# One-bank attention steps held back and issued ahead of a three-bank step, in a two-layer hybrid encoder kernel on one core

## The chip, the core and the metric

The kernel runs on one core of a Trainium2 chip. The metric is device time in microseconds (us) of one execution, and the time of a kernel is the median of several. Five engines work side by side and each takes its own instructions in program order: PE (matrix products and transposes), DVE (vector work), ACT (scalar functions and copies), POOL and SP (which starts most transfers). Results of PE land in PSUM, which has eight banks.

## What is computed

Two layers run over 320 tokens: 256 of a prompt and the next 64 of a stream with a cache. Each layer has one combined projection, two kinds of attention of eight heads each, an output projection and a feed-forward block:

```
h   = x @ w_in                      # q, k, v of A and of B, and an indexer's q, k, w
A   = softmax(q k' / 8 + bias) v    # band of 64-frame chunks, learned relative bias
B   = the same over the 64 (prompt) or 80 (sample) keys that the indexer picks:
      score[t,s] = sum_h w[t,h] * relu(q_idx[t,h] . k_idx[s]),  top k of the admissible keys
x   = LayerNorm(alpha * x + concat(A, B) @ w_out)
x   = LayerNorm(alpha * x + relu(x @ w_up)^2 @ w_down)
```

All is float32. The outputs are the 320 rows of x and the new keys, values and indexer keys of both layers.

## The kernel before, in words

**Weight products.** Every weight arrives as units of 1024 x 128 numbers (`raw`, loaded by SP). ACT rounds a unit to a high part (`wh`, L184) and DVE subtracts it to get the low part (`wl`, L190). Tokens are split in the same way, and for each unit and each of eight slices of 128 inputs PE issues three products (L202, L203, L204: high x high, high x low, low x high) over all 320 tokens into a bank of a pool `mm`. There are 4776 of them. "Product 480" below means the point in PE's order after 480 of these, counted from the start of the program.

**Attention steps.** Each layer has eight pairs of heads, four of A (the code calls them with `flip`, or b0 to b3 in the output's order) and four of B. When the projections of a pair are there, its steps follow one another:

- value: three transposes (L333) into one bank, two copies by ACT (L334, L335).
- scores: six products (L399, L401) into three banks; DVE adds the bias and takes maxima (L419, L422); ACT takes exponentials (L427, "exps"); DVE and ACT divide by the sums (L432, L435, L437).
- turn: nine transposes (L451) into three banks, copied out by ACT (L455, L457, L458) or DVE (L453).
- output: twelve small products (L470, L473) into one bank, which the step finish empties: ACT rounds (L479), DVE subtracts (L480).
- dots and weigh (L541, L543, L518, L520) score keys for the indexer; DVE picks the best (L583, L585). Keys and queries of B are rotated by DVE first (L302 to L305).

These steps share a pool `at` of four banks, taken in turn, so that a step's bank is free once the reader of the bank's last user is done.

**What sets the order.** The program is written by a planner in Python, before anything runs. It has a clock that goes forward by 0.408 us after each three products. `later(dt, fn)` puts a step on an agenda at clock + dt with dt from a table WAIT (for layer 0, output 2.0, finish 4.0, value 5.2; for layer 1, 3.8, 3.2 and 9.2), and `advance` issues what is due, oldest first. A step that finds too few banks by the planner's count (`held`) is put off to the next slot. Issuing a step appends its instructions to the order of each engine that it uses: so the place of L479 in ACT's order and of L480 in DVE's follows from when the planner issues finish, and finish is due a fixed time after its output.

```
        later(WAIT[l]["finish"], self.finish, p)
...
        nc.scalar.activation(self.o[0], pv, AF.Copy)
        nc.vector.tensor_tensor(self.o[1], pv, self.o[0].bitcast(F32), op=ALU.subtract)
        release(1)
```

Of the kernel before, what the change touches and what calls it, by code (L numbers as in the profile page):

```python
# [44 lines left out]
N_WARM = 6  # L45
N_TAIL = 4
STORE = 10.0
TOKENS = slice(0, P), slice(P, 2 * P), slice(T - P, T)
WAIT = [{"lo": 3.4, "rope": 4.6, "scores": 3.4, "peaks": 0.0, "exps": 1.0, "normalise": 5.6, "turn": 3.0,
         "output": 2.0, "finish": 4.0, "value": 5.2, "keys": 6.0, "dots": 10.8, "clip": 0.0, "weigh": 0.2,  # L50
# [25 lines left out]
def encoder_step(ctx: ExitStack, tc: tile.TileContext, a: dict):  # L76
# [24 lines left out]
    held = [0]  # L101

    def side_banks(n, fn, *args):

        if held[0] + n > N_SIDE:
            later(NEXT, fn, *args)
            return None
        held[0] += n
        return [acc("at", N_SIDE) for _ in range(n)]

    def release(n):
        held[0] -= n

    def unit(dt=F32, w=T):
        return st([P, 3 * P], "u", N_UNIT, dt)[:, :w]
# [5 lines left out]
    clock = [0.0]  # L121
    agenda = []

    def later(dt, fn, *args):
        agenda.append((clock[0] + dt, len(agenda), fn, args))

    def advance(dt):
        clock[0] += dt
        while agenda:
            i = min(range(len(agenda)), key=lambda i: agenda[i][0])  # L130
            if agenda[i][0] > clock[0]:
                break
            _, _, fn, args = agenda.pop(i)
            fn(*args)

    def put(out, t):

        later(STORE, nc.sync.dma_start, out, t)

    def flush():  # L140
        while agenda:
            advance(NEXT)


# [29 lines left out]
    def prefetch(upto):  # L174

        while at["split"] <= min(upto, len(units) - 1):
            i = at["split"]
            while i not in raw:
                advance(NEXT)
            w = raw.pop(i)  # L180
            n = w.shape[2]
            hi = st([P, KD, P], "wh", 5, F32R)[:, :, :n]
            lo = st([P, KD, P], "wl", 5, F32R)[:, :, :n]
            nc.scalar.activation(hi, w, AF.Copy)  # L184
            split[i] = (hi, lo)
            at["split"] += 1
            later(WAIT[l]["lo"], split_rest, i, hi, lo, w)
# [7 lines left out]
    def until(ready):  # L195
        while not ready():
            advance(NEXT)
# [93 lines left out]
    def evacuate(dst, src, scale=1.0):  # L291
        s, b = src
        if b is None:
            nc.scalar.activation(dst, s, AF.Copy, scale=scale)  # L294
        elif scale != 1.0:
            nc.vector.tensor_scalar(dst, s, b, scale, op0=ALU.add, op1=ALU.mult)
        else:
            nc.scalar.activation(dst, s, AF.Identity, bias=b, scale=scale)
# [21 lines left out]
    def value(v, src, out, then):  # L320

        f = unit()
        evacuate(f, src)
        put(out, f)

        def turn():
            got = side_banks(1, turn)
            if not got:
                return
            pt = got[0]  # L330
            release(1)
            for c, n in ((0, P), (1, P), (2, TS)):
                nc.tensor.transpose(pt[:n, c * P:(c + 1) * P], f[:, c * P:c * P + n], ident)  # L333
            nc.scalar.activation(v[:, 0:2], pt[:, 0:2 * P].rearrange("p (c d) -> p c d", c=2), AF.Copy)  # L334
            nc.scalar.activation(v[:TS, 2], pt[:TS, 2 * P:3 * P], AF.Copy)  # L335
            then()

        later(WAIT[l]["value"], turn)

    def bias_tiles(l, j):  # L340

# [9 lines left out]
    def sample_blocks(f, at, keep):  # L351

        other = f[:, (at + 64 if keep == 0 else at - 64):][:, :64]
        here = f[:, at:at + 64]
        mine, rest = HALVES[keep][1], HALVES[1 - keep][1]
        nc.gpsimd.tensor_copy(other[rest], here[rest])
        nc.gpsimd.memset(here[rest], 0.0)
        nc.gpsimd.memset(other[mine], 0.0)

    class Pair:  # L360
# [18 lines left out]
        def got(self, what):  # L379
            self.have.add(what)  # L380
            if what == "q":
                sample_blocks(self.qf, 64 if self.flip else 2 * P, 1 if self.flip else 0)
            if what in "qk" and {"q", "k"} <= self.have:
                later(WAIT[l]["scores"], self.scores)
            if {"v", "p"} <= self.have:
                later(WAIT[l]["output"], self.output)

        def scores(self):
            if not self.add:
# [41 lines left out]
        def normalise(self):  # L431
            nc.vector.reciprocal(self.sums, self.sums)  # L432
            for i, (p, _, _) in enumerate(self.parts):
                if i < WAIT[l]["na" if self.flip else "nb"]:
                    nc.scalar.activation(p, p, AF.Copy, scale=self.sums[:, i:i + 1])  # L435
                else:
                    nc.vector.tensor_scalar(p, p, self.sums[:, i:i + 1], None, op0=ALU.mult)  # L437
            later(WAIT[l]["turn_a" if self.flip else "turn"], self.turn)

        def turn(self):  # L440
            banks = side_banks(3, self.turn)
# [42 lines left out]
    class Index:  # L484
# [40 lines left out]

        def got(self, j):
            sample_blocks(self.qf[j], 2 * P, 0)
            later(WAIT[l]["dots"], self.dots, j)

        def dots(self, j):  # L530

# [139 lines left out]
    class LastNorm(Norm):  # L671
# [20 lines left out]
        def finish(self, psum):  # L692
# [13 lines left out]
            def gather(c0, part, first=False, last=False):  # L706

                for i, t in enumerate(TOKENS):
                    nc.tensor.matmul(pc[:, c0 + i:c0 + i + 1], part[:, t], mean_w[:, 0:1], start=first and i == 0,
# [47 lines left out]
    for l in range(DEPTH):  # L757
# [4 lines left out]
        def take(name, j, src):  # L762
            if name == "ki":
                index.keys(src)
            elif name == "qi":
                roped(index.q[j], src, 0, None, lambda: index.got(j))
            else:
                p, kind, br = pairs[name[1], j], name[0], name[1]
                if kind == "v":
                    value(p.v, src, a["o_" + name][l, j], lambda: p.got("v"))  # L770
                elif br == "b":
                    roped(getattr(p, kind), src, 2 if kind == "q" else 0, a["o_kb"][l, j] if kind == "k" else None,
                          lambda: p.got(kind))
                elif kind == "q":
                    evacuate(p.q, (src[0][:, T - 1::-1], src[1]), scale=HD ** -0.5)
                    later(WAIT[l]["a"] - WAIT[l]["scores"] if kind == "k" else 0, p.got, kind)
                else:
                    evacuate(p.k, src)
                    put(a["o_ka"][l, j], p.k)
                    later(WAIT[l]["a"] - WAIT[l]["scores"] if kind == "k" else 0, p.got, kind)  # L780
# [68 lines left out]
        if not final:  # L849
# [9 lines left out]
            for k in range(0, KD, 2):  # L859
                later(WAIT[l]["renew"] + WAIT[l]["renew2"] * k, renew, k)  # L860
    flush()


# [88 lines left out]
```

## Time and profile before

| | before |
|---|---|
| median of 3 executions | 825.57 us (825.29 to 828.98) |
| the profiled execution | 827.0 us, span 824.2 us |
| PE busy | 815.2 us, 99% of the span |
| DVE busy | 604.5 us, 73% |
| ACT busy | 446.3 us, 54% |
| granted PE clock | full (1.00) in every stretch listed below |

The profile is of one execution; its span runs from the first to the last instruction, and the time lies 2.8 us above it. Busy shares are means over stages that differ much: DVE stands near 100% in some stretches of the attention and near 40% in the feed-forward blocks. The chain that ended last lies 93% on PE.

### The profile page before, as it was taken

Reading aid. Unit: us, or ns where it says so; the run is one execution under the profiler, and the core shown is the slowest. Engines: PE = TensorE matmul, PEld = TensorE weight load, DVE = VectorE, ACT = ScalarE, POOL = GpSimd, SP = SyncE. Lnnn points to the kernel's source line nnn. Section 1 sums busy time; section 2 is a strip of 40 time slices with the busy share of each in tenths; the row PEclk is TensorE's granted clock in tenths of the full one; section 3 lists DMA queues with packets and bytes.
Section 4 is the critical chain, followed back from the end, with each engine's and each line's share of the span. In section 5 each row is a group of like instructions: output and inputs, shape, how many; then the busy total and the mean of one; then the engine's idle time right before and its main releaser. Section 6 shows DMA issues by size and latency. Waiting matters only on the chain.

```text
span 824.2 us, 14973 instructions
## 1 busy us (share of the span) xinstructions
PE 815.2 (99%) x5790; PEld 791.2 (96%) x5790; DVE 604.5 (73%) x1335; ACT 446.3 (54%) x848; POOL 71.5 (9%) x227
## 2 busy tenths in 40 slices
PE   8999999999999999999999999999999999999997
PEld 8899999999999999999999999889999999999995
DVE  4978887587988875364597799987699888545343
ACT  5566666546655544344367646585466555444332
POOL 0451110010000000000521211100000000000000
PEclk9999999999999999999999999999999999999998
DMA  9785344164444444444776343342435343534301
GB/s 344 194 238 188 136 133 141 62 172 156 153 154 153 153 154 155 153 146 161 187 165 228 119 140 123 119 136 103 154 107 179 136 145 151 196 111 165 142 1 64
DMA packets 27016, 124.04 MB, mean 151 GB/s; under 512 B 4993, under 2 KB 11521, under 8 KB 14402
## 3 DMA queue, kind: packets, MB, share of 16 engines
q1 hardware_dynamic: 23234, 113.84, 39.6%
q0 software_dynamic: 3424, 8.92, 5.5%
q8 instruction: 45, 0.74, 0.4%
q10 hardware_dynamic: 288, 0.34, 0.1%
q14 instruction: 25, 0.20, 0.1%
HBM read 116.36 MB, written 6.72 MB: 149 GB/s over the span
## 4 chain that ended last, share of the span: by engine, by line
PE 93%; DVE 4%; DMA 2%; ACT 0%; issue 0%
PE mm L202 28%; PE mm L203 27%; PE mm L204 27%; PE at L451 2%; PE at L399 1%; PE at L470 1%; PE at L401 1%; DMA raw<-w_all 1%; DMA u<-w_first 1%; DVE u L585 1%; DVE wl L190 1%; PE at L541 1%; DVE m L583 1%; PE at L543 1%; PE at L333 1%; PE at L473 1%
## 5 line engine op out<-in xcount | busy, mean ns | idle before, releaser
L202 PE MATMUL mm<-u,wh 128*128 128x320 f32 x1024 | 320.9, 313 | 1.9 <-ACT u L294 1.9
L204 PE MATMUL mm<-u,wl 128*128 128x320 f32 x1024 | 316.5, 309 | 0.0
L203 PE MATMUL mm<-u,wh 128*128 128x320 f32 x1024 | 316.3, 309 | 0.0
L184 ACT ACTIVATE wh<-raw 128x1024 fp32r<-128x1024 f32 x199 | 209.2, 1053 | 143.6 <-PE mm L203 130.5
L190 DVE TENSOR_TENSOR wl<-raw,wh 128x1024 fp32r<-128x1024 f32 x199 | 241.2, 1218 | 47.0 <-ACT wh L184 46.7
L202 PEld LDWEIGHTS mm<-u,wh 128*128 128x128 f32 x1024 | 192.0, 187 | 2.9 <-ACT u L294 2.2
L203 PEld LDWEIGHTS mm<-u,wh 128*128 128x128 f32 x1024 | 192.0, 188 | 0.0
L204 PEld LDWEIGHTS mm<-u,wl 128*128 128x128 f32 x1024 | 191.8, 187 | 0.1
L202 PE MATMUL mm<-rh,wh 128*128 128x322 f32 x568 | 177.4, 312 | 0.0
L203 PE MATMUL mm<-rl,wh 128*128 128x322 f32 x568 | 176.5, 311 | 0.0
L204 PE MATMUL mm<-rh,wl 128*128 128x322 f32 x568 | 176.3, 310 | 0.0
L203 PEld LDWEIGHTS mm<-rl,wh 128*128 128x128 f32 x568 | 107.7, 190 | 0.2
L202 PEld LDWEIGHTS mm<-rh,wh 128*128 128x128 f32 x568 | 107.5, 189 | 0.2
L204 PEld LDWEIGHTS mm<-rh,wl 128*128 128x128 f32 x568 | 107.4, 189 | 0.0
L611 DVE SCALAR_TENSOR_TENSOR x<-x,mm 128x320 f32<-128x320 f32 x31 | 15.0, 487 | 80.0 <-PE mm L204 80.0
L819 ACT ACTIVATE z<-z,c 128x320 f32<-128x320 f32 x64 | 36.1, 563 | 32.4 <-DVE z L282 32.4
L280 DVE SCALAR_TENSOR_TENSOR z<-mu,mm 128x320 f32<-128x320 f32 x71 | 38.7, 545 | 13.1 <-PE mm L204 13.1
L348 POOL DMA_DIRECT2D u<-rel x48 | 25.8, 541 | 226.3 <-PE mm L204 212.5
L427 ACT ACTIVATE u<-u,mx 128x128 f32<-128x128 f32 (+2 forms) x80 | 37.0, 464 | 11.7 <-DVE mx L422 11.5
L613 ACT ACTIVATE rh<-x,ln 128x320 fp32r<-128x320 f32 x24 | 13.5, 563 | 48.3 <-DVE x L611 48.3
L294 ACT ACTIVATE u<-mm 128x320 f32<-128x320 f32 (+1 forms) x51 | 21.8, 430 | 28.4 <-PE mm L204 26.9
L826 DVE TENSOR_TENSOR u<-h,u 128x320 fp32r<-128x320 f32 x64 | 31.5, 493 | 6.7
(145 smaller groups left out, 777.0 us busy)
## 6 DMA issues: line engine op xcount, KB each, us to landing
raw<-w_all SPq DMA_DIRECT2D x98, 1024.0 KB, 4.9
u<-rel POOLq DMA_DIRECT2D x16, 128.0 KB, 6.1
u<-rel POOLq DMA_DIRECT2D x16, 80.0 KB, 6.6
o_va<-u SPq DMA_DIRECT2D x8, 160.0 KB, 5.8
o_ka<-u SPq DMA_DIRECT2D x8, 160.0 KB, 5.8
o_kb<-u SPq DMA_DIRECT2D x8, 160.0 KB, 5.1
o_vb<-u SPq DMA_DIRECT2D x8, 160.0 KB, 5.4
o_y<-x SPq DMA_DIRECT2D x8, 160.0 KB, 1.9
```

The source lines that it names most:

```text
L184: nc.scalar.activation(hi, w, AF.Copy)
L190: nc.vector.tensor_tensor(lo, w, hi.bitcast(F32), op=ALU.subtract)
L202: nc.tensor.matmul(out, hi[:, k], xh, start=first, stop=False)
L203: nc.tensor.matmul(out, hi[:, k], xl, start=False, stop=False)
L204: nc.tensor.matmul(out, lo[:, k], xh, start=False, stop=last)
L280: nc.vector.scalar_tensor_tensor(u, mu[:n], p[:, T:T + 1], p[:, :T], op0=ALU.mult, op1=ALU.add)
L294: nc.scalar.activation(dst, s, AF.Copy, scale=scale)
L348: nc.gpsimd.dma_start(dst, bass.AP(tensor=e.tensor, offset=off + at0, ap=[[1, n], [1, m]]))
L427: nc.scalar.activation(p, p, AF.Exp, bias=self.mx[:, i:i + 1], scale=1.0, accum_out=self.sums[:, i:i + 1])
L451: nc.tensor.transpose(t[:n, c * P:(c + 1) * P], p[:, c * P:c * P + n], ident)
L819: nc.scalar.activation(u, u, AF.Relu, bias=b)
L826: nc.vector.tensor_tensor(hl, h, hh.bitcast(F32), op=ALU.subtract)
```

## The change

Value and output, the two steps that take one bank, no longer go onto the agenda's own due time. When due they are put on a list `riders` with a deadline 10 planner-microseconds later (HOLD; some 73 products). The steps that take three banks (scores, turn, dots) are issued through `lead`, which first issues the oldest rider if no bank is held, and then the step. A rider past its deadline is issued by `advance`, as are all that are left when the agenda is empty.

```
+HOLD = 10.0
...
             fn(*args)
+        while riders and (riders[0][0] <= clock[0] or not agenda):
+            _, fn, args = riders.pop(0)
+            fn(*args)
...
+    riders = []
+
+    def ride(dt, fn, *args):
+        later(dt, riders.append, (clock[0] + dt + HOLD, fn, args))
+
+    def lead(fn, *args):
+
+        if riders and not held[0]:
+            _, first, more = riders.pop(0)
+            first(*more)
+        fn(*args)
...
-        while agenda:
+        while agenda or riders:
             advance(NEXT)
...
-        later(WAIT[l]["value"], turn)
+        ride(WAIT[l]["value"], turn)
...
-                later(WAIT[l]["scores"], self.scores)
+                later(WAIT[l]["scores"], lead, self.scores)
             if {"v", "p"} <= self.have:
-                later(WAIT[l]["output"], self.output)
+                ride(WAIT[l]["output"], self.output)
...
-            later(WAIT[l]["turn_a" if self.flip else "turn"], self.turn)
+            later(WAIT[l]["turn_a" if self.flip else "turn"], lead, self.turn)
...
-            later(WAIT[l]["dots"], self.dots, j)
+            later(WAIT[l]["dots"], lead, self.dots, j)
```

Every engine has as many instructions as before; POOL's and SP's orders are the same. On PE, the groups of attention steps that stand between products fall from 58 to 46 (those before the first products and after the last ones counted). Moved are, by product number: in layer 0 the value transposes of 159, 207, 255, 279, 591, 615 and 639 (now at 165, 237, 303, 318, 618 and, two of them, 648) and the outputs of 318, 366, 447, 495 and 630 (now at 351, 432, 480, 522 and 648); in layer 1 the value transposes of 2451, 2472, 2496 and 2520 (now at 2526, 2541, 2571 and 2589), one of 3069 (now 3072) and the outputs of 2928 and 2976 (now 2946 and 2997). Product 648 and product 3072 are the ends of the layers' input projections, where output products wait for the last attention step. Line numbers of the changed program are higher by 17 from L150 on: L496 there is L479 here, L497 is L480, L444 is L427, L350 is L333.

**ACT near product 366 (at 92 to 96 us of the trace before).** The exponentials of the scores of product 366 (L427, u_1262 to u_1264; in the change L444, u_1247 to u_1249), and L479 of the output (u_438 at 366 before, u_379 at 351 in the change). Before:

```order
111 L435 ACTIVATE u_1104<-u_1104,sums_1107 128x128
112 L427 ACTIVATE u_1262,sums_1266<-u_1262,mx_1265 128x128
...
116 L427 ACTIVATE u_1264,sums_1266<-u_1264,mx_1265 128x320
117 L294 ACTIVATE u_1311<-mm_1228 128x320
118 L184 ACTIVATE wh_1323<-raw_1168 128x1024
119 L479 ACTIVATE u_438<-at_1249 128x320
```

In the change:

```order
110 L452 ACTIVATE u_1091<-u_1091,sums_1094 128x128
111 L444 ACTIVATE u_1247,sums_1251<-u_1247,mx_1250 128x128
...
115 L444 ACTIVATE u_1249,sums_1251<-u_1249,mx_1250 128x320
116 L496 ACTIVATE u_379<-at_1170 128x320
117 L311 ACTIVATE u_1298<-mm_1226 128x320
118 L201 ACTIVATE wh_1310<-raw_1155 128x1024
```

The finish of the output that stood at product 318, whose L479 came long before these rows, now has its L479 right behind the five exponentials; that of the output of 366 has left this place for a later one.

**DVE at the same place.** L422 (L439) ends the maxima that these exponentials wait for, L432 and L437 divide for an earlier pair, L583 picks keys. Before:

```order
173 L422 TENSOR_SCALAR mx_1265<-mx_1265 128x5
174 L432 RECIPROCAL sums_1107<-sums_1107 128x5
175 L437 TENSOR_SCALAR u_1104<-u_1104,sums_1107 128x256
176 L437 TENSOR_SCALAR u_1105<-u_1105,sums_1107 128x320
177 L583 MAX m_269_1299<-u_360 128x8
```

In the change:

```order
172 L439 TENSOR_SCALAR mx_1250<-mx_1250 128x5
173 L449 RECIPROCAL sums_1094<-sums_1094 128x5
174 L454 TENSOR_SCALAR u_1091<-u_1091,sums_1094 128x256
175 L454 TENSOR_SCALAR u_1092<-u_1092,sums_1094 128x320
176 L497 TENSOR_TENSOR u_380<-at_1170,u_379 128x320
177 L600 MAX m_268_1286<-u_360 128x8
```

L480 (here L497), which needs the L479 of the rows above, now stands ahead of the picking.

**ACT at the start of layer 1 (near product 2526 to 2541).** L298 moves one projection into place, L334 and L335 copy value transposes (L315, L351 and L352 in the change). Before:

```order
410 L298 ACTIVATE u_4790<-z_5142,c_5141 128x320
411 L334 ACTIVATE u_4980<-at_5177 128x256
412 L335 ACTIVATE u_4980<-at_5177 64x128
413 L184 ACTIVATE wh_5188<-raw_5105 128x1024
414 L298 ACTIVATE u_4979<-z_5184,c_5183 128x320
415 L294 ACTIVATE u_4978<-mm_5191 128x320
```

In the change:

```order
405 L201 ACTIVATE wh_5164<-raw_5093 128x1024
406 L315 ACTIVATE u_4979<-z_5160,c_5159 128x320
407 L351 ACTIVATE u_4791<-at_5179 128x256
408 L352 ACTIVATE u_4791<-at_5179 64x128
409 L351 ACTIVATE u_4844<-at_5200 128x256
410 L352 ACTIVATE u_4844<-at_5200 64x128
411 L311 ACTIVATE u_4978<-mm_5167 128x320
```

The copies of the value transposes at product 2526 (bank at_5179) now stand behind the L298 of u_4979. The scores of product 2541 take three banks, and the third is the one that at_5179 used.

## Rows read from the trace of the kernel before

**Rows 1.** What PE waited for: us in total, times, longest us (the longest entry).

```profile
PE mm L202 <- ACT u L294: 1.9, 1, 1.9
```

**Rows 2.** Busy time by stretch: PE, PEld, DVE, ACT, POOL; PEclk, DMA share, GB/s.

```profile
91.90:111.90 20.00, 20.00 (x164) 19.21 (x161) 19.65 (x62) 12.83 (x39) 3.77 (x14) 1.00 0.43 141
...
484.00:552.00 68.00, 67.07 (x518) 62.13 (x517) 66.31 (x234) 42.77 (x122) 8.67 (x30) 1.00 0.42 137
```

**Rows 3.** PE's timeline, 105 to 148 us: start, duration, what.

```profile
105.23 0.93 PE L399 MATMUL at<-u,u 64*128 64x128 f32 x8
...
112.98 1.14 PE L451 MATMUL at<-ident,u 128*128 128x128 f32 x9
113.88 0.39 PE L202 MATMUL mm<-u,wh 128*128 128x320 f32 x1
...
123.12 1.14 PE L451 MATMUL at<-ident,u 128*128 128x128 f32 x9
...
147.17 0.41 PE L202 MATMUL mm<-u,wh 128*128 128x320 f32 x1
147.43 0.30 PE L203 MATMUL mm<-u,wh 128*128 128x320 f32 x1
```

**Rows 4.** DVE's timeline, 92 to 114 us (brackets: idle before, what ended it).

```profile
92.94 1.01 DVE L583 MAX8 m<-u 128x8 f32<-128x128 f32 x3
...
97.84 0.49 DVE L480 TENSOR_TENSOR u<-at,u 128x320 fp32r<-128x320 f32 x1
98.25 1.22 DVE L190 TENSOR_TENSOR wl<-raw,wh 128x1024 fp32r<-128x1024 f32 x1
...
102.48 0.49 DVE L305 TENSOR_TENSOR u<-u,u 128x320 f32<-128x320 f32 x1
...
107.25 0.28 DVE L419 CUSTOM_DVE_ANT_0 u<-at,u 128x128 f32<-128x128 f32 x1
...
108.89 0.17 DVE L422 TENSOR_SCALAR mx<-mx 128x5 f32<-128x5 f32 x1
...
110.12 0.51 DVE L302 STREAM_SHUFFLE u<-u 128x320 f32<-128x320 f32 x1
...
111.44 0.49 DVE L305 TENSOR_TENSOR u<-u,u 128x320 f32<-128x320 f32 x1
113.13 0.49 DVE L480 TENSOR_TENSOR u<-at,u 128x320 fp32r<-128x320 f32 x1 [1.20 <-ACT u L479]
```

**Rows 5.** ACT's timeline, 95 to 113 us.

```profile
95.74 0.41 ACT L294 ACTIVATE u<-mm 128x320 f32<-128x320 f32 x1
...
109.09 0.40 ACT L427 ACTIVATE u<-u,mx 128x128 f32<-128x128 f32 x1 [4.05 <-DVE mx L422]
...
111.42 0.41 ACT L294 ACTIVATE u<-mm 128x320 f32<-128x320 f32 x1
...
112.68 0.42 ACT L479 ACTIVATE u<-at 128x320 fp32r<-128x320 f32 x1
```

**Rows 6.** DVE, then PE, at 523 to 527 us: two waits of PE for DVE.

```profile
523.36 0.49 DVE L305 TENSOR_TENSOR u<-u,u 128x320 f32<-128x320 f32 x1
...
526.40 0.48 DVE L480 TENSOR_TENSOR u<-at,u 128x320 fp32r<-128x320 f32 x1
...
524.00 0.93 PE L399 MATMUL at<-u,u 64*128 64x128 f32 x8 [0.21 <-DVE u L305]
...
526.93 0.88 PE L470 MATMUL at<-u,u 128*64 128x128 f32 x12 [0.72 <-DVE u L480]
```

**Rows 7.** The start of layer 1: ACT, then PE.

```profile
436.16 0.56 ACT L298 ACTIVATE u<-z,c 128x320 f32<-128x320 f32 x1 [0.72 <-DVE z L282]
...
437.05 1.05 ACT L184 ACTIVATE wh<-raw 128x1024 fp32r<-128x1024 f32 x1
438.29 0.56 ACT L298 ACTIVATE u<-z,c 128x320 f32<-128x320 f32 x1 [0.18 <-DVE z L282]
...
439.05 0.87 PE L401 MATMUL at<-u,u 128*128 128x256 f32 x4
```

## Prediction

> **What bounds the kernel now.** I read the waits of PE first. Only one entry is above 1 us, the 1.9 us of [rows 1], once and before the attention steps concern us; so PE has nearly no slack, and whatever makes it wait comes on top of the time. Second, the busy time by stretch [rows 2]: PE is busy without a gap from 91.9 to 111.9 us, and DVE is busy 19.65 of the same 20.00 us. In layer 1, from 484 to 552, DVE is busy 66.31 of 68.00. In such stretches DVE has no reserve: a delay on it is carried along until DVE next waits for something. The reader should see two engines that are full at once: PE sets the time, and DVE is close behind it. Third, the timelines of DVE, ACT and PE around one attention step, to see what is waited for in each engine's order.
>
> **The change, part by part.** It removes, adds and lengthens no instruction. It moves some twenty steps, and with them, in the orders of ACT and DVE, the copies of value and the finish of output. No transfer is moved past another: SP's and POOL's orders stay.
>
> *Fewer interruptions (a gain).* A product's row lasts 0.30 (147.43); the first product behind an output run lasts 0.41 (147.17), the one behind a turn 0.39 (113.88) [rows 3]. So leaving a run costs about 0.11 more than a product does. I let entering one cost as much again, at most; a joined pair saves one way in and one way out, at most 0.22. Twelve runs disappear: the gain is 12 x 0.22 = 2.6 us at most, and nothing at least, since a step can also lose where kinds of operands change. Value transposes and turns are transposes like each other and enter without much of a gap; half of the twelve are such. I take 0.05 to 0.1 for each, about 0.9 us in all, 0.6 of it in layer 0, where it counts; the 0.3 of layer 1 falls where DVE is full and sets the pace, and I count it as nothing.
>
> *The finish of an output, late behind exponentials (a loss, layer 0).* This is what the orders shown for ACT and DVE do. The output of product 318 now stands at 351. Its L479 comes right behind the five exponentials of the scores of 366, at the place where L294 is at 95.74 [rows 5]. Its L480 stands on DVE ahead of the picking, which before began at 92.94 [rows 4]. From L479 to L480 it takes 0.45 (112.68 in [rows 5], 113.13 in [rows 4]), so L480 starts at 96.19. The picking starts 0.41 later (97.84 to 98.25, the pitch of an L480), at 96.60: 3.66 late. One L480 later in this stretch (97.84) is no longer there, which gives 0.41 back: DVE is 3.25 us late, and full [rows 2]. That DVE does stand for an L479 is seen in the trace: it was idle 1.20 before 113.13. The Trainium skill, "PSUM — Partial Sum Buffer", section "Engine vs sequencer instructions", says that the queues of ScalarE and VectorE are strict FIFO; by that rule no later work of DVE can slip past a waiting L480, and the idle 1.20 agrees. If instead independent work could pass, the sum would lose the next three terms.
>
> First, the rotation that ends with the L305 of 102.48 ends 3.25 later, starting at 105.73. The scores of product 447 need it. From L305 to the scores that wait for it are 0.64 us (523.36 to 524.00, [rows 6]), so they start at 106.37 and not at 105.23 [rows 3]: **1.14**.
>
> Second, L422 of these scores moves from 108.89 to 112.14. The first exponential follows L422 by 0.20 (109.09), the five take 2.33 (to 111.42), and what stands between them and L479 takes 1.26 (to 112.68) [rows 5]. In the change this L479 is that of the output of 432 and starts at 112.14 + 0.20 + 2.33 + 1.26 = 115.93; its L480 at 116.38. The turn of product 480 needs that bank as its third. From L480 to the PE step that waits for it are 0.53 (526.40 to 526.93, [rows 6]): 116.91. Without this wait the turn would start at 112.98 + 1.14 (an output of about 1.3 us leaves the scores ahead of it and returns just in front of it, so the two cancel), and its third bank 0.60 later, two thirds of the 0.90 from 112.98 to 113.88 [rows 3]: 114.72. The difference is **2.2**.
>
> Third, the same once more. From L480 at 116.38 DVE has an L480 (0.41), two rotations (1.73 each: 110.12 to 111.44, and 0.41), an L190 (1.14: 1.22 less the 0.08 by which rows overlap on DVE) and the maxima (1.64: 107.25 to 108.89): L422 at 123.03 [rows 4]. There a normalising copy of ACT stands ahead of the exponentials; I add an estimate of 0.45 for it (an ACT row of that size lasts 0.40, [rows 5]). Then 0.45 + 0.20 + 2.33 + 1.26 and again 0.45 give L480 at 127.72, and the third bank of the turn of product 522 at 128.25, against 123.12 + 1.14 + 2.2 + 0.60 = 127.06: **1.2**.
>
> A fourth such place, a rotation for the scores of 591, comes out at about **0.3** by the same count. The sum is 4.8. Its floor is 0, if the planner's later steps find slack that I don't see; its ceiling is what DVE loses at the first two places, if all of it reaches PE: 3.25, and 3.0 where DVE is through with its L190 at 112.14 + 1.22 and then stands to 116.38, with the 1.2 and 0.3 behind them 7.8.
>
> *The end of layer 0's projection (a loss).* At 648 five one-bank steps and two are now left over, and the output whose result the next products read first comes last. Its L479 and L480 are then exposed: 0.45 + 0.53 behind PE's last product of it, which the output behind it covered before (an output takes some 1.3). I take 1.1 with a copy of the turn that is 0.26 late, and 0 to 1.5 for the range.
>
> *The start of layer 1 (a loss).* Four value steps leave the products up to 2520, and PE comes earlier to the scores of 2541. But their third bank is that of the value step now at 2526, whose copies stand behind the L298 of 438.29, which waits for DVE [rows 7]. From an L298 through both copies takes 0.89 (436.16 to 437.05). The bank is free at 439.18, and with some 0.15 to PE its third-bank products start at 439.33; before they did at 439.05. PE is 0.28 late there although two value steps (0.3 each, three transposes at the 0.1 of a turn's nine) are still to come: 0.28 + 0.66 = **0.9**. Floor: 0 if PE's head start is kept, ceiling 1.2.
>
> *The rest of layer 1.* Outputs 2928 and 2976 move by some twenty products. By the order their L480 stands where the L479 is already done (behind an L190 that covers it), so DVE does not stand longer. I count nothing.
>
> Sum: 4.8 + 1.1 + 0.9 - 0.6 = +6.2 us. The profiled execution took 827.0, so such a one would take 833.2; against the median of 825.57 it is 831.8. A measurement here tells about 0.5%, or 4.1 us, from no change.
>
> **The rivals.** *The blocks are absorbed, and nothing is seen.* For it: 3.25 us on DVE become only 1.14 on PE at the first place, so rotations are needed late; one idle stretch of 1.2 us that stays would take up part of the rest. Against it: in [rows 2] there is 0.35 us of reserve in 20. Then the ends remain, +1.1 + 0.9 - 0.6, some of it gone as well: about +1, **826.5**, within 825.3 to 828.5.
>
> *The change pays.* The place is the edge of each run on PE. If edges cost the full 0.22, and no L480 is waited for, 12 x 0.22 = 2.6 less: **823.0**. It decides itself at the scores of 447: if they start when their products are done, this is the case. Against it are the orders, in which L479 does stand behind the exponentials. Even so it would stay within 0.5%; 4.1 us less would need more than the edges hold.
>
> *It costs more, in layer 1.* If L480 blocks DVE there as in layer 0, by 3 us at each of two outputs where DVE is full [rows 2], that comes wholly on top: 831.8 + 6 = **838**. Against it is the order just named.
>
> *The change joins little*, since a held bank forbids it. It joins 12 of 58; this is counted above.
>
> **How the numbers follow.** My sum: 0.54. Absorbed: 0.32. It pays: 0.05. More in layer 1: 0.09 (half of it short of 836). The predicted time is that of the sum, 831.8, its own range 829 to 834.5. The range for 8 in 10 takes in the absorbed case from 825.3 and the sum's own ceiling of the blocks: 825.3 to 835.5. Faster by over 0.5% (below 821.4) has no mechanism of its own: 0.04. Slower by over 0.5% (above 829.7) holds the sum, less its lower end, and the dear case: 0.57. The same: 0.39.
>
> **What the profile of the changed kernel would show.** Right: entries of PE's waits "L451 <- DVE L480" of some 2 us and 1.2 us, and "L399 <- DVE L305" of 1 us; DVE idle about 3 us ahead of an L480, released by ACT's L479, near 96 and 116 us; at layer 1's start a wait of the L401 products for ACT's L335, of 0.9. Wrong: no such waits, or DVE's idle there no longer than 1.2; then something released L479 earlier than the order lets me see. It would also be wrong if a wait in layer 1 longer than 1 us appears that I did not place.

## The result, and the profile after

The changed kernel takes 833.07 us (median of 7, 829.45 to 835.23), the kernel before 826.66 us (median of 7, 824.87 to 829.93). The ratio is 1.0073, with a 95% interval of 1.0055 to 1.0092: slower by 4.5 to 7.6 us, 6.0 in the middle. The forecast was +6.2 us.

PE's waits in the changed kernel, us in total, times, longest (L468 is the L451 of before, L416 is L399, L497 is L480, L322 is L305):

```profile
PE at L468 <- DVE u L497: 2.9, 2, 2.0
PE at L416 <- DVE u L322: 1.3, 2, 1.1
PE mm L219 <- ACT u L311: 1.2, 1, 1.2
PE mm L255 <- POOL mean_w L232: 1.0, 1, 1.0
PE at L418 <- issue: 1.0, 1, 1.0
PE mm L219 <- ACT u L496: 0.5, 1, 0.5
PE at L487 <- DVE u L497: 0.5, 1, 0.5
...
```

Before, only the start-up's entry was above 1 us [rows 1]; here it is the third, at 1.2. The new ones are at the four places that the prediction named: the turns that wait for L480, the scores that wait for a rotation (1.1 of the 1.3), the third bank at the start of layer 1 (L418, put down to "issue", of which more below), and the first products of the next part behind L479 (L496) at the end of layer 0.

The timelines of the changed kernel at the same places as [rows 3 to 5] and [rows 7], DVE first, then ACT, then PE:

```profile
88.72 0.29 DVE L436 CUSTOM_DVE_ANT_0 u<-at,u 128x128 f32<-128x128 f32 x1 [2.91 <-PE at L416]
...
94.47 0.49 DVE L497 TENSOR_TENSOR u<-at,u 128x320 fp32r<-128x320 f32 x1 [3.16 <-ACT u L496]
94.88 1.01 DVE L600 MAX8 m<-u 128x8 f32<-128x128 f32 x3
...
104.01 0.49 DVE L322 TENSOR_TENSOR u<-u,u 128x320 f32<-128x320 f32 x1
...
110.43 0.17 DVE L439 TENSOR_SCALAR mx<-mx 128x5 f32<-128x5 f32 x1
...
114.66 0.49 DVE L497 TENSOR_TENSOR u<-at,u 128x320 fp32r<-128x320 f32 x1 [2.93 <-ACT u L496]
...
125.99 0.49 DVE L497 TENSOR_TENSOR u<-at,u 128x320 fp32r<-128x320 f32 x1 [2.14 <-ACT u L496]
```

```profile
93.48 0.55 ACT L444 ACTIVATE u<-u,mx 128x320 f32<-128x320 f32 x1
94.02 0.41 ACT L496 ACTIVATE u<-at 128x320 fp32r<-128x320 f32 x1
...
114.21 0.42 ACT L496 ACTIVATE u<-at 128x320 fp32r<-128x320 f32 x1
...
441.56 0.56 ACT L315 ACTIVATE u<-z,c 128x320 f32<-128x320 f32 x1 [0.61 <-DVE z L299]
442.03 0.36 ACT L351 ACTIVATE u<-at 128x256 f32<-128x256 f32 x1
442.29 0.26 ACT L352 ACTIVATE u<-at 64x128 f32<-64x128 f32 x1
```

```profile
104.65 0.93 PE L416 MATMUL at<-u,u 64*128 64x128 f32 x8 [1.05 <-DVE u L322]
...
112.35 0.88 PE L468 MATMUL at<-ident,u 128*128 128x128 f32 x6
115.21 0.55 PE L468 MATMUL at<-ident,u 128*128 128x128 f32 x3 [1.99 <-DVE u L497]
...
124.70 0.87 PE L468 MATMUL at<-ident,u 128*128 128x128 f32 x6
126.54 0.55 PE L468 MATMUL at<-ident,u 128*128 128x128 f32 x3 [0.96 <-DVE u L497]
...
152.53 0.97 PE L350 MATMUL at<-ident,u 128*128 128x128 f32 x6
...
158.20 0.41 PE L219 MATMUL mm<-u,wh 128*128 128x320 f32 x1 [0.54 <-ACT u L496]
...
442.65 0.84 PE L418 MATMUL at<-u,u 128*128 128x256 f32 x4 [0.95 <-issue]
```

What the reader is to see: the last exponential at 93.48, L479 (L496) right behind it at 94.02, and DVE, which had stood idle 3.16 us, starting L480 (L497) 0.45 later, with the picking behind it. The rotation's last step at 104.01 is 0.64 ahead of the scores at 104.65. The turn of product 480 has its first two banks filled from 112.35, then stands 1.99 us for L480 of 114.66 and goes on 0.55 behind it. At 442.65 the third bank of the scores follows L352 of 442.29: I read "issue" in that row as the wait for this copy, which the profile did not attribute (e5_no_values_in_layer_1 tests it).

Product 140 starts at 41.31 us here and at 43.03 in the trace before, so 1.72 us set one clock to the other. With them added, the rows of 94.47, 94.88, 104.01, 104.65, 110.43, 114.66 and 125.99 stand at 96.19, 96.60, 105.73, 106.37, 112.15, 116.38 and 127.71; the prediction's count had 96.19, 96.60, 105.73, 106.37, 112.14, 116.38 and 127.72.

**Where the time went, product by product.** The two kernels issue the same 4776 products in the same order, so the start of the n-th in one trace can be set against that in the other. The table is worked out so: start of product n less start of product 140 (no step was moved before it), in each trace, and the difference to the kernel before, in us. Where a kernel has not yet issued a step that the other has, the figure is lower by that step: at 447 all kernels whose outputs ride owe one output, 1.3 us.

```
kernel                     447    485    525    700   2592   4775
the change               -0.14  +3.35  +4.54  +4.99  +5.95  +5.60
e1_values_only           +0.06  +0.06  +0.06  +1.93  +2.90  +3.01
e2_outputs_only          -0.12  +3.35  +4.55  +4.19  +4.18  +3.74
e3_finish_early          -1.26  +0.03  +0.04  +0.23  +1.21  +0.85
e7_round_early           -1.26  +0.03  +0.04  +0.23  +1.19  +0.83
e8_rest_late             -1.26  +0.84  -0.45  +0.91  +1.86  +1.49
e5_no_values_in_layer_1  -1.26  +0.03  +0.04  +0.23  +0.24  -0.21
e6_outputs_finish_early  -1.24  +0.04  +0.05  -0.43  -0.43  -0.90
e4_before_finish_early   +0.00  +0.00  +0.48  +0.82  +0.82  +0.82
```

(e8 owes one output at 525.) The profiled execution of the change has a span only 3.1 us longer than before, not 5.6: it reached product 140 at 41.31 us, the kernel before at 43.03, with the same instructions up to there, and what follows the last product took 13.5 us against 14.2. It is also the fastest of the seven. The granted clock is no part of these differences: from 45 to 805 us it is 1.00 in all ten profiled executions.

### The profile page after: what moved, and what is told of

Read it like the earlier page. It is cut to its first block, busy times and chain, and to the rows that moved or that the text cites. A ratio compares the mean times of both kernels' runs of the same rounds, so it can differ in the third digit from the quotient of the medians.

```text
span 827.3 us, 14977 instructions
## 1 busy us (share of the span) xinstructions
PE 813.8 (98%) x5790; PEld 789.5 (95%) x5790; DVE 604.3 (73%) x1335; ACT 445.8 (54%) x848; POOL 73.5 (9%) x227
## 4 chain that ended last, share of the span: by engine, by line
PE 87%; DVE 8%; ACT 2%; DMA 2%; issue 1%; ACTq 0%; DVEq 0%
PE mm L219 26%; PE mm L220 26%; PE mm L221 26%; DVE wl L207 2%; PE at L468 1%; DVE u L602 1%; DVE m L600 1%; PE at L416 1%; DMA raw<-w_all 1%; PE at L487 1%; PE at L418 1%; DVE u L436 1%; DMA u<-w_first 1%; PE at L558 1%; PE at L560 1%
## 5 line engine op out<-in xcount | busy, mean ns | idle before, releaser
L444 ACT ACTIVATE u<-u,mx 128x128 f32<-128x128 f32 (+2 forms) x80 | 37.0, 464 | 13.1 <-DVE mx L439 11.9
L630 ACT ACTIVATE rh<-x,ln 128x320 fp32r<-128x320 f32 x24 | 13.5, 563 | 49.3 <-DVE x L628 49.3
```

Of the source, the lines that this page charges most:

```text
L444: nc.scalar.activation(p, p, AF.Exp, bias=self.mx[:, i:i + 1], scale=1.0, accum_out=self.sums[:, i:i + 1])
```

## The experiments

Two theories were to be told apart. Mine: DVE stands for an L479 that was put behind exponentials, and what DVE then delivers late, PE waits for. Rivals: joined runs or the steps' new places on PE cost by themselves (the bank that an output takes just ahead of a turn), whatever finish does. All ratios below are to the kernel before on the same chip, with 95% intervals.

**e1_values_only**

```
             if {"v", "p"} <= self.have:
-                ride(WAIT[l]["output"], self.output)
+                later(WAIT[l]["output"], self.output)
```

> Only the value steps ride; outputs are issued when due, as before. My theory (DVE stands for an L479 behind exponentials): the waits of the turns at 480 and 522 and of the scores at 447 are gone, product 522 comes within 0.5 us of its place before; the wait at the start of layer 1 (third bank of the scores at 2541) stays, about 1 us. In all 0.5 to 1.5 us slower than before. Rival (joined runs cost PE by themselves, whichever step rides): about half of the loss stays, 3 us slower.

Measured: 1.0028 (1.0013 to 1.0044); by the traces +3.01 us. That total is the rival's number and not mine, but not where the rival has it: the attention of layer 0 up to product 525 is at its place before within 0.06 us, as the theory says, and the start of layer 1 costs 0.97 (from 700 to 2592). At the end of layer 0 it loses 1.87, which neither theory had. PE's timeline there in this kernel (L487 is L470, L350 is L333, L351 is L334):

```profile
151.53 0.55 PE L350 MATMUL at<-ident,u 128*128 128x128 f32 x3
152.55 0.88 PE L487 MATMUL at<-u,u 128*64 128x128 f32 x12 [0.47 <-ACT u L351]
153.26 0.52 PE L490 MATMUL at<-u,u 128*64 128x64 f32 x12
153.70 0.55 PE L350 MATMUL at<-ident,u 128*128 128x128 f32 x3
154.72 0.88 PE L487 MATMUL at<-u,u 128*64 128x128 f32 x12 [0.47 <-ACT u L351]
155.43 0.52 PE L490 MATMUL at<-u,u 128*64 128x64 f32 x12
156.48 0.41 PE L219 MATMUL mm<-u,wh 128*128 128x320 f32 x1 [0.54 <-ACT u L496]
```

Two held values are issued singly in front of the outputs that use them, and each of these outputs waits for its value's copy. The three waits are 1.48 of the 1.87.

**e2_outputs_only**

```
-        ride(WAIT[l]["value"], turn)
+        later(WAIT[l]["value"], turn)
```

> Only the outputs ride; values are issued when due, as before. Theory: all of layer 0's loss stays, product 522 about 4.5 us later than before, and the start of layer 1 loses nothing: 4.5 to 5.5 us slower in all. Rival (joined runs cost by themselves): about 3 us slower, and some of the layer 0 loss gone with the values.

Measured: 1.0032 (1.0017 to 1.0046), and by the traces +3.74 us. Up to 525 it loses 4.55, the change 4.54: the outputs are the whole of that loss, and nothing of it goes with the values, as the rival had it. The total is below the 4.5 to 5.5 that I expected because two places gain: 0.36 from 525 to 700, and 0.44 from 2592 to the end. Nothing is lost at the start of layer 1.

**e3_finish_early**

```
-         "output": 2.0, "finish": 4.0, "value": 5.2, "keys": 6.0, "dots": 10.8, "clip": 0.0, "weigh": 0.2,
+         "output": 2.0, "finish": 2.0, "value": 5.2, "keys": 6.0, "dots": 10.8, "clip": 0.0, "weigh": 0.2,
```

> The whole change, with WAIT's finish of layer 0 at 2.0 and not 4.0: PE's order stays that of the change, step for step, but L479 and L480 of the outputs at 351, 432, 480 and 522 stand ahead of the exponentials and maxima of the next scores. Theory: DVE no longer stands 3 us for L479, product 522 comes within 0.7 us of before, and what stays is the end of layer 0 (0.5) and the start of layer 1 (1.0): 1 to 2 us slower than before. Rival (an output just ahead of a turn takes the turn's third bank, wherever finish stands): the turn still waits for L480, two waits of 1 to 2 us; 4 us slower or more.

Measured: 1.0000 (0.9982 to 1.0018). With PE's order unchanged step for step, product 525 is at +0.04 and not at +4.54; what stays is 0.19 at the end of layer 0 and 0.98 at the start of layer 1, less 0.36 in the rest of layer 1: 0.85 in all, where I expected 1 to 2, and the medians show no difference. So the new places of the steps on PE cost nothing by themselves in that stretch, and the rival falls. One row shows that standing alone is no loss: on DVE here

```profile
92.17 0.49 DVE L497 TENSOR_TENSOR u<-at,u 128x320 fp32r<-128x320 f32 x1 [2.86 <-ACT u L496]
```

DVE stands 2.86 for the first L479, at a place where in the change it stood 2.91 for the scores anyhow (88.72 above).

**e7_round_early**: L479 early, L480 where the change has it (at the first output it stands behind the picking, not ahead of it).

```
         def finish(self, p):
...
             nc.scalar.activation(self.o[0], pv, AF.Copy)
-            nc.vector.tensor_tensor(self.o[1], pv, self.o[0].bitcast(F32), op=ALU.subtract)
-            release(1)
-            self.done = True
+
+            def rest():
+                nc.vector.tensor_tensor(self.o[1], pv, self.o[0].bitcast(F32), op=ALU.subtract)
+                release(1)
+                self.done = True
+
+            later(2.0 if l == 0 else 0.0, rest)
...
-         "output": 2.0, "finish": 4.0, "value": 5.2, "keys": 6.0, "dots": 10.8, "clip": 0.0, "weigh": 0.2,
+         "output": 2.0, "finish": 2.0, "value": 5.2, "keys": 6.0, "dots": 10.8, "clip": 0.0, "weigh": 0.2,
```

> The whole change, with finish cut in two in layer 0: L479 at 2.0 after the output, L480 where the change has it (4.0). PE's order stays that of the change. DVE reaches L480 at the same place of its order, but L479 is no longer behind the exponentials. Theory (the cost is DVE standing for L479): no standing of 2 to 3 us, product 522 at its place before within 0.5 us, as in e3_finish_early. Rival (the cost is the late place of L480 itself, which gives the bank back late): the turns at 480 and 522 still wait 1 to 2 us for L480.

Measured: 0.9999 (0.9986 to 1.0013), product 525 at +0.04. ACT, DVE and PE of this kernel:

```profile
88.82 0.43 ACT L496 ACTIVATE u<-at 128x320 fp32r<-128x320 f32 x1
...
112.76 0.88 ACT L472 ACTIVATE u<-at 128x384 f32<-128x384 f32 x2 [1.11 <-PE at L468]
...
93.85 0.48 DVE L499 TENSOR_TENSOR u<-at,u 128x320 fp32r<-128x320 f32 x1
...
104.14 0.93 PE L416 MATMUL at<-u,u 64*128 64x128 f32 x8
...
111.84 1.20 PE L468 MATMUL at<-ident,u 128*128 128x128 f32 x9
...
121.99 1.20 PE L468 MATMUL at<-ident,u 128*128 128x128 f32 x9
...
148.53 0.82 PE L350 MATMUL at<-ident,u 128*128 128x128 f32 x6
```

L480 (L499) follows L479 by 5 us and waits for nothing, and both turns go through in one piece. DVE no longer stands for L479 there, and the loss is gone with it: 4.50 of the 4.54 at product 525.

**e8_rest_late**: the same cut, with finish left at 4.0, so that L479 stays behind the exponentials and L480 comes 2.0 later.

> The whole change, with finish cut in two in layer 0 the other way: L479 where the change has it, behind the exponentials, L480 2.0 later, behind picking and a rotation. PE's order stays that of the change up to product 522 (the output of 495 then goes ahead of the scores of 543). Theory (DVE standing): DVE finds L479 done, or stands 1.2 us as before; the scores of 447 start on time and the turn of 480 waits 0 to 0.5 us; product 485 is 3 us earlier than in the change. Rival (a bank given back late): the turn of 480 waits 2 us or more, since the bank comes back later still.

Measured: 1.0030 (1.0009 to 1.0051). The scores of 447 are on time (-1.26 at 447), and product 485 is 2.51 us earlier than in the change (0.84 against 3.35; I expected 3): most of the loss goes although L479 stands behind the exponentials as in the change. But the turn of 480 waits more than the theory let it. DVE, ACT and PE:

```profile
111.67 0.49 DVE L499 TENSOR_TENSOR u<-at,u 128x320 fp32r<-128x320 f32 x1 [1.20 <-ACT u L496]
...
112.40 0.88 ACT L472 ACTIVATE u<-at 128x384 f32<-128x384 f32 x2 [0.77 <-PE at L468]
...
111.48 0.88 PE L468 MATMUL at<-ident,u 128*128 128x128 f32 x6
112.95 0.55 PE L468 MATMUL at<-ident,u 128*128 128x128 f32 x3 [0.59 <-ACT u L472]
```

DVE stands 1.20, as in [rows 4]; the turn's third bank comes 0.8 late (I expected a wait of 0 to 0.5), and the profile names a copy of ACT, L472 (the L455 of before). That copy is not late because of L479. ACT had stood idle 0.77 before it, for the turn itself, and it starts 0.92 behind the turn's start (111.48 to 112.40), just as in e7_round_early, where L479 is early (111.84 to 112.76). It is the copy of this turn's own first tile: in the program built from this kernel the turn's third tile lies in the bank of its first, while in the change and in e7_round_early it lies in the bank of the output of 432. (So the four banks are not taken strictly in turn, as the kernel was described above.) What the 0.8 shows is a turn that had only two banks to itself, not a price of a late L479; why the program got this bank is not shown. The whole is +1.49 against +0.83 in e7_round_early: this 0.8, less 0.15 because the output of 495 now goes ahead of the scores of 543.

**e5_no_values_in_layer_1** is e3_finish_early with

```
-        ride(WAIT[l]["value"], turn)
+        (ride if l == 0 else later)(WAIT[l]["value"], turn)
```

> The kernel of e3_finish_early, and the values of layer 1 issued when due. Theory: the wait of 1 us for L335 at the start of layer 1 is gone and nothing else changes: 1 us faster than e3_finish_early, so 0 to 1 us slower than before. Rival (DVE, full there, holds PE whatever the values do): no difference to e3_finish_early.

Measured: 0.9990 (0.9975 to 1.0005). From 700 to 2592 it loses 0.01, e3_finish_early 0.98. ACT and PE at that place:

```profile
437.46 0.56 ACT L315 ACTIVATE u<-z,c 128x320 f32<-128x320 f32 x1 [0.19 <-DVE z L299]
...
438.21 0.87 PE L418 MATMUL at<-u,u 128*128 128x256 f32 x4
```

No copy of a value stands behind L298 (L315) now, and the third bank is not waited for. So "issue" in the change was the wait for that copy.

**e4_before_finish_early**: the kernel before, no riders, with finish of layer 0 at 2.0.

> The kernel before (no riders) with layer 0's finish at 2.0. That puts L479 of the outputs of 318 and 366 right behind the exponentials and moves L480 of those of 447 and 495 ahead of a rotation, so that DVE stands there about as long as in the change (3 us). Theory: DVE stands, but no turn waits for these banks, and only what DVE delivers late can reach PE: 0 to 1.5 us slower, without a wait of a turn for L480. Rival (DVE standing 3 us always reaches PE): 3 us slower or more.

Measured: 0.9998 (0.9983 to 1.0013); by the traces +0.82 us. DVE, then PE:

```profile
112.65 0.49 DVE L480 TENSOR_TENSOR u<-at,u 128x320 fp32r<-128x320 f32 x1 [2.94 <-ACT u L479]
123.99 0.49 DVE L480 TENSOR_TENSOR u<-at,u 128x320 fp32r<-128x320 f32 x1 [2.15 <-ACT u L479]
...
115.03 0.93 PE L399 MATMUL at<-u,u 64*128 64x128 f32 x8 [0.40 <-DVE u L305]
126.36 0.93 PE L399 MATMUL at<-u,u 64*128 64x128 f32 x8 [0.24 <-DVE u L305]
```

DVE stands as long as in the change at its second and third place, but here no turn waits for the bank, and only 0.40 and 0.24 of it reach PE by these rows (0.47 and 0.35 product by product). So some 3 us of standing are worth what waits behind them: 0.5 here, 1.1 at the scores of 447 in the change, 2.2 where a turn's third bank hangs on that L480.

**e6_outputs_finish_early**: e3_finish_early with the values issued when due in both layers; the parts that the runs above show to cost nothing.

> Only the outputs ride, and layer 0's finish is 2.0: the parts that cost nothing by the runs so far. Theory: no wait of a turn for L480, none at the start of layer 1; counted from product 24 to the last, 0.8 to 1.0 us less than before (0.4 at the end of layer 0, 0.4 at 2997 of layer 1), which lies at the edge of what five rounds tell: 0.999. Rival (a joined run pays nothing): 1.000, and no place earlier than before.

Measured: 0.9988 (0.9973 to 1.0003), 825.88 us against 827.06. By the traces it gains 0.48 at the end of layer 0 and 0.47 in layer 1, 0.90 in all. Its list of waits:

```profile
PE mm L219 <- ACT u L311: 1.7, 1, 1.7
PE mm L255 <- POOL mean_w L232: 1.0, 1, 1.0
PE at L487 <- DVE u L497: 0.5, 1, 0.5
...
```

The medians don't tell it from the kernel before, nor from e5_no_values_in_layer_1. Its ratio is the lowest of those tried; by the traces it is 0.9 us ahead, 0.1%.

## Why the prediction was right, and where its sizes were off

**The block on DVE.** Right in mechanism, place and size. DVE stood 3.16 and 2.93 us at the first two outputs; the count had 3.25 of delay at the one and 3.0 of standing at the other. Against e7_round_early, which has the same order on PE, the scores of 447 lost 1.13 (forecast 1.14), the turn of 480 then 2.19 (2.2), the turn of 522 1.18 (1.2). The fourth place, the scores of 591, was put at 0.3; between products 590 and 610 the change lost 0.1 more than e7_round_early. Sum 4.6 for 4.8. The picking at 94.88, which needs nothing of that L480, began only behind it. The Trainium skill, "PSUM — Partial Sum Buffer", section "Engine vs sequencer instructions", states that ScalarE's and VectorE's queues are strict FIFO, and this trace agrees.

**The end of layer 0.** Forecast +1.1 for the exposed finish and -0.6 for joins, +0.5 in all. Measured from 525 to 700 is +0.45, of which 0.1 belongs to the fourth place: 0.35. That it came so near is luck, for both parts were too large. The wait behind the last output is there, but it is 0.54: the products begin once L479 is done, and the count let them wait for L480 too. (Its parts, 0.45, 0.53 and 0.26, also add up to 1.24 and not to 1.1.) The six value transposes of 152.53 take 0.97 against 0.82 in e7_round_early, another 0.15. The rest, -0.34, I put down to joining. That the wait comes from held values is shown by e2_outputs_only and e6_outputs_finish_early, which have none and gain 0.36 and 0.48 there.

**The joins in the attention of layer 0.** I had 0.6 of gain in layer 0, at 0.05 to 0.1 for each run that disappears. Up to product 525 four runs disappear (20 become 16), and nothing is gained: e3_finish_early and e7_round_early are at +0.04 there. The four are value steps, put ahead of dots, scores or a turn. Counted as in the table above, at the place that a step leaves and at the place where it arrives, a value step gives back 0.33 and costs 0.33 again: joining it pays nothing. The outputs of 318, 366, 447 and 495 took no run away. They stood behind scores in the kernel before, so a pair was only exchanged for another: an output costs 1.27 behind scores and 1.30 ahead of a turn. Alone it costs 1.35, and ahead of scores 1.15 (e8_rest_late at 543). So I mis-sized this term by one price for every join; what a join pays depends on which step goes ahead of which.

**The start of layer 1.** Forecast 0.9, measured 0.96 (700 to 2592), all of it the wait of 0.95 for the third bank, and gone in e5_no_values_in_layer_1.

**The rest of layer 1.** Forecast nothing, with the reason that DVE is full there and sets the pace. Measured -0.35 from 2592 to the end, and -0.44 and -0.47 in e2_outputs_only and e6_outputs_finish_early. The wait of 0.72 in [rows 6] became 0.52 there (0.5 in the list of waits above), and the output that now goes ahead of the scores of 2997 saves most of the rest. So DVE, though busy 66.31 of 68.00 us [rows 2], did not set the pace of PE there: that assumption was wrong, at a price of 0.4.

Sum by the traces: 4.6 + 0.35 + 0.96 - 0.35 = 5.6 for the forecast 6.2. The large term is right for its own reason; that the small ones add up so well (+1.0 for a forecast of +1.4) owes something to errors that cancel. The absorbed case, the rival with 0.32, did not come: none of the 1.14, 2.2 and 1.2 was taken up again. The dear case in layer 1 did not either: the L480 of the two outputs that moved there do not wait for L479, before or after.

## What to carry to other kernels

When a step moves, follow what it issues on the other engines: here the step on PE was free to move, and its two small followers on ACT and DVE, which a planner issues a fixed time later, landed behind five exponentials and made a full engine stand. Price such standing by what is queued behind it and when that is wanted: some 3 us cost 2.2 where a turn's bank hung on them, 1.1 and 0.5 where a rotation did. And price a join by the pair that it makes, from rows of such pairs, not by the number of runs that disappear: here a value step gained nothing from being joined, and an output 0.05 ahead of a turn and 0.2 ahead of scores.

## What was not expected of the hardware

From product 140 on, two kernels with the same order over a stretch agree to 0.02 us over hundreds of products (e3_finish_early and e7_round_early at 447, 485, 525 and 700), while the stretch before it, the same instructions in all kernels, differs from one execution to the next: product 140 is reached at 41.31 us in the change, 43.03 before and 44.81 in e3_finish_early. So one pair of profiles, aligned at such a product, told terms of 0.1 us apart that medians with intervals of 1 to 2 us on either side did not.
